# A streaming encoder step on one core: attention blocks transposed into other PSUM tiles, half of the weight differences on GpSimd, other steps and banks at the ends of the state-space loop

## The chip, the cores and the metric

The kernel is one program on one core of a Trainium2 chip. Its time is the device time of one execution in microseconds; the figure given for a version is the median of several executions. The engines are TensorE (PE, with its weight loads shown apart as PEld), VectorE (DVE), ScalarE (ACT), GpSimd (POOL) and SyncE (SP), which here issues nearly all DMAs. Each engine runs its own instructions strictly in the order of the program; a waiting instruction holds all behind it on its engine.

## The reference

It is one layer of a hybrid encoder, for 2048 frames of a new stream and 8 x 16 frames of running streams (17 tiles of 128 frames), in float32:

```
h = rms_norm(x) * gain
u, g_s, q, k, v, g_a = split(h @ w_in)            # w_in: 1024 x 3072
y_s = S5(u): 32 groups of 16 channels, each with a 64-dim complex diagonal state,
      a scan over the frames, y = Re(C h) + D u, gelu, then a GLU with w_glu (512 x 1024)
y_a = band attention: 8 heads x 64, q and k normed, each chunk of 64 frames sees itself
      and the 8 chunks before, bias by clipped distance; running streams attend a cache of 512
mixed = concat(y_s * silu(g_s), y_a * silu(g_a))
out = x + mixed @ w_out                           # w_out: 1024 x 1024
```

Returned are the outputs, the newest keys and values, and the final states.

## The kernel before

**Two streams of work.** `run` interleaves a foreground (the input projection `inproj` in three passes over the 17 tiles, then `glu`, then `outproj`) and a background (preparation of the state-space part, `s5`, `decode` for the running streams, `attention`). All are Python generators that write instructions as they go; each `yield` states a cost. For each foreground cost (650 for a step of three matmuls) the background earns that cost times a ratio (0.42 while `s5` runs, 0.75 in `decode`; in `attention` it is worked out so that it ends 64 steps before the foreground) and spends it on its own yields. While a burst of weight conversions is due (`busy`), the ratio is 0. So the order of instructions on each engine is fixed when the program is written, and a yield of the background is a count of foreground steps put between two of its pieces.

**Matmuls in three terms.** Each product of the foreground (`mm3`, lines 190 to 194) takes a float32 operand as a rounded high part and a low difference: high x high, high x low, low x high. The weights go through `conv_w` (line 145 on): a block of 128 x 512 is loaded by SP into one of five raw buffers (`NR`), ACT writes the rounded part `whi` (line 155, scaled by the norm's gain), DVE the difference `wlo` (line 156). The blocks of pass 1 and pass 2 are converted in a burst at the last tile of the pass before, 16 blocks at 1.25 steps each, and the load of the block five further on is issued two steps later (`T_LW`). Their first use is one step per block from the start of the new pass.

**q and k.** `ev_norm` has DVE sum the squares (`s`, line 280), POOL make a reciprocal root from it (lines 281 and 282), DVE scale (`zs`, line 285), and PE transpose the result into a PSUM tile `tr` (line 295). The one buffer of `tr` in the pool `pst` also holds the transposes of `glu` (line 1361).

**The state-space loop.** `s5` loads blocks of u (`load_u`, SP), reorders them on ACT (`perm_u`, line 720) and transposes them on PE (`step_a`, line 734); `feed(n)` loads block n+3, reorders block n+1 and transposes block n. The first of these follow the flag that pass 0 has stored u. In the loop DVE and ACT rotate and scan, POOL makes tables of cosines and sines, PE multiplies. At its end PE transposes the final states into a PSUM tile `ut` with one buffer, DVE copies them out (line 938) into a buffer `bt` with one, and SP stores them, behind eight stores of y (line 850).

**Attention.** 128 pieces: 16 units of two heads and four frames' tiles, two heads each, four tiles of queries. `qk` multiplies into the PSUM tile `s` and DVE adds the bias and takes the minimum; `soft` makes exponentials on ACT; `tr` transposes the weights by PE in blocks of 128 (up to five, line 1203) into the PSUM tile `pt`, which holds 8 blocks, two banks, one buffer; ACT writes their rounded part (`pth`, line 1210), DVE the difference (`ptl`, line 1211); `pv` multiplies with the values. Every fourth piece from the 12th on also brings a gate: `gate_b` transposes two blocks into the last two places of `pt`, and DVE multiplies (`mo`, line 1256). The list `post` holds DVE work back until the next yield is over. The PSUM pools of attention have one buffer for each tag (`bufs=1` is the default of `pool`), and with `s` (two banks), `pt` (two), `o` (one), `tr` (one) and the foreground's two all eight banks are in use.

**Glu.** For each tile SP loads the stored gate `gs` (line 1376), POOL multiplies it into `ms` (line 1402), and PE transposes that one tile later (line 1361).

Of the kernel before, what the change touches and what calls it, by code (L numbers as in the profile page):

```python
# [31 lines left out]
def fv(ap):  # L32
    return ap.bitcast(F32)
# [6 lines left out]
class Build:  # L40
# [101 lines left out]
    def conv_w(self):  # L142
        nc = self.nc
        n = self.nconv
        self.nconv += 1
        key, _, k = self.chunks[n]
        raw = self.raws.pop(n)
        hi = self.wp.tile([128, 512], F32R, tag="whi", name="whi", bufs=16)
        lo = self.wp.tile([128, 512], F32R, tag="wlo", name="wlo", bufs=16)
        if k is None:  # L150
            nc.scalar.activation(out=hi, in_=raw, func=AF.Copy)
            nc.vector.tensor_sub(lo, raw, fv(hi))
        else:
            gcol = self.gain[:, k:k + 1]
            nc.scalar.activation(out=hi, in_=raw, func=AF.Copy, scale=gcol)  # L155
            nc.vector.scalar_tensor_tensor(lo, raw, gcol, fv(hi), op0=OP.mult, op1=OP.subtract)  # L156
        self.W[key] = (hi, lo)
        if self.step:
            self.defer(self.T_LW, lambda: self.load_w(n + self.NR))
        elif n + self.NR < 16:  # L160
            self.load_w(n + self.NR)
        else:

            self.defer(40 + 10 * (n + self.NR - 16), lambda: self.load_w(n + self.NR))
# [286 lines left out]
    def s5(self):  # L451
# [257 lines left out]
        def load_u(b, i):  # L709
            c0, n = BLK[i]  # L710
            u = mp.tile([128, L, GB * CH], F32, tag="U", name="U", bufs=3)
            nc.sync.dma_start(u[0:n], u4[c0:c0 + n, :, b * GB * CH:(b + 1) * GB * CH])
            U[b, i] = u

        def perm_u(b, i):
            n = BLK[i][1]
            u = U.pop((b, i))
            o = mp.tile([128, GB, L, CH], F32, tag="P", name="P")
            src = u[0:n].rearrange("p j (g h) -> p g j h", g=GB)
            nc.scalar.activation(out=o[0:n], in_=src, func=AF.Copy)  # L720
            P[b, i] = o.rearrange("p g j h -> p g (j h)")
# [148 lines left out]
            yield None  # L870
        for n in range(3):
            load_u(0, n)
        yield 2 * SL
        perm_u(0, 0)
        yield SL
        for n in range(3):
            feed(n)
            yield SL
# [52 lines left out]
        nc.sync.dma_start(self.O["rp"], of[:, 0:64])  # L931
        nc.sync.dma_start(self.O["ip"], of[:, 64:128])
        for i in range(2):
            yield 1500
            pf = ps.tile([128, 128], F32, tag="ut", name="pf2")
            nc.tensor.transpose(pf, FINs[:, 4 * i:4 * i + 4].rearrange("p b g -> p (b g)"), self.ident)
            of = mp.tile([128, 128], F32, tag="bt", name="of2", bufs=1)
            nc.vector.tensor_copy(of, pf)
            nc.sync.dma_start(self.O["rs"][128 * i:128 * i + 128], of[:, 0:64])
            nc.sync.dma_start(self.O["is"][128 * i:128 * i + 128], of[:, 64:128])  # L940
# [163 lines left out]
    def attention(self):  # L1104
# [91 lines left out]
        def tr(x, gate):  # L1196
            n, s, a = x
            j0 = span(x)
            w = a + 5 - j0
            pr = PR.pop(x)  # L1200
            t = ps.tile([128, 8, 128], F32, tag="pt", name="pt")
            for k in range(w):
                nc.tensor.transpose(t[:, k], pr[:, 128 * k:128 * k + 128], self.ident)  # L1203
            if gate is not None:
                gate_b(gate, t[:, 6:8])
            if a == 0:
                PT[n, s] = [p.tile([128, 20, 128], F32R, tag=f"pt{y}", name=f"pt{y}", bufs=1) for y in "hl"]

            h, l = (v[:, 4 * a + j0:5 * a + 5] for v in PT[n, s])
            nc.scalar.activation(out=h, in_=t[:, 0:w], func=AF.Copy)  # L1210
            post.append(lambda: nc.vector.tensor_tensor(out=l, in0=t[:, 0:w], in1=fv(h), op=OP.subtract))  # L1211

        def pv(n, s, y):
            if y == 0:
# [26 lines left out]
        def gate_b(gate, t):  # L1241
            n, h = gate
            m, G = units[n]
            for a in range(2):
                nc.tensor.transpose(t[:, a], GT[n][:, 2 * h + a], self.ident)
            o = p.tile([128, 2, 128], F32, tag="mo", name="mo")
            ot = OT[n]
            P = 2 * G + h

            def put():  # L1250
                nc.sync.dma_start(self.mt_d[2 * P:2 * P + 2, :, 4 + m, :].rearrange("t p q -> p t q"), o)
                if m == 3:
                    self.flags["att", P] = True

            def mul():
                nc.vector.tensor_mul(o, ot[:, 2 * h:2 * h + 2], t)
                late.append(put)

            post.append(mul)

        subs = [(n, s, a) for n in range(len(units)) for s in range(2) for a in range(4)]
        SL = self.SL_ATT
# [18 lines left out]
        for i in range(N + 6):  # L1281
            self.att_left = N + 6 - i
            if i < N:
                x = subs[i]
                while not self.flags.get(("ga", 4 * units[x[0]][1] + 3)):
                    yield None
                qk(x)
                yield self.W_QT * SL
                flush()
            done = i >= 2 and subs[i - 2][2] == 3 if i - 2 < N else False  # L1290
            if done:
                n, s, a = subs[i - 2]
                pv(n, s, 0)
                if i < N:
                    soft(x)
                yield self.W_PV * SL
                flush()
                pv(n, s, 1)
                yield self.W_PV * SL
                flush()  # L1300

            gate = None
            if i % 4 == 0 and i >= 12 and i < N:
                gate = (i - 12) // 8, (i - 12) // 4 % 2
            elif i in tail:
                gate = tail[i]
            if 0 <= i - 1 < N:
                tr(subs[i - 1], gate)
                gate = None
                yield self.W_QT * SL  # L1310
                flush()
                self.use_spare()
            if gate is not None:
                gate_b(gate, ps.tile([128, 8, 128], F32, tag="pt", name="pt")[:, 6:8])
                yield self.W_QT * SL
                flush()
            if i < N and not done:
                soft(x)
            if i >= 8 and i % 8 == 0:
                gate_a(i // 8 - 1)  # L1320
            if i < N:
                n, r = x[0], i % 8
                if r == 2:
                    load_ga(n)
                if n + 1 < len(units) and r < 6:
                    loads(n + 1)[r]()
                if r == 3:
                    bias(2 * n + 2)
                if r == 5:
                    bias(2 * n + 3)  # L1330
# [22 lines left out]
    def glu(self):  # L1353
# [13 lines left out]
        for i, t in enumerate(TILES):  # L1367
# [5 lines left out]
                self.out_load(0)  # L1373
            hi, lo = self.GY.pop(t)
            g = self.ev.tile([128, 512], F32, tag="plain", name="gs")
            nc.sync.dma_start(g, self.gs_d[128 * t:128 * t + 128])
            z = {}
            for f in (1, 0):
                z[f] = self.psm.tile([128, 512], F32, tag="mm", name="z")
# [229 lines left out]
```

## Time and profile before

| | |
|---|---|
| median of 3 executions | 1228.99 us (1226.14 to 1230.14) |
| profiled execution | 1225.45 us, its span 1223.6 us |
| mean granted TensorE clock | 0.993 |
| PE busy | 97% |
| DVE busy | 58% |
| ACT busy | 50% |
| POOL busy | 30% |
| DMA, mean | 194 GB/s |

The profile is that of one execution. Busy time is the union of an engine's instructions; matmuls overlap in the pipeline and their ends are modelled, so a matmul is shown longer than the distance to the next one. "Idle before" is the time in which an engine did nothing ahead of an instruction, with what ended it. The granted clock is the share of TensorE's full clock that was given in a stretch.

### The profile page before, as it was taken

The numbers are of one execution on the slowest core, as the hardware profiler recorded it, in microseconds if no ns is written. First come the engines' busy times: TensorE is split into PE (matmuls) and PEld (weight loads), VectorE is DVE, ScalarE is ACT, GpSimd is POOL, SyncE is SP. The second block draws the span as 40 slices with busy tenths as digits, with TensorE's granted clock in tenths as the row PEclk, the third lists the DMA queues.
The fourth block names the chain that finished last, engine by engine and source line by source line (L and its number), as shares of the span: only waits on it lengthen the run. The fifth ranks groups of instructions, "written<-read, shape, count | busy, mean of one in ns | idle before, by whom it ended". The sixth has DMA issues, their size and how long they took to land.

```text
span 1223.6 us, 18141 instructions
## 1 busy us (share of the span) xinstructions
PE 1185.6 (97%) x6363; PEld 973.3 (80%) x6363; DVE 714.5 (58%) x1358; ACT 610.6 (50%) x1177; POOL 364.2 (30%) x407
## 2 busy tenths in 40 slices
PE   8999999899999999999899999999999999999998
PEld 6888888678788887787667878788788788888887
DVE  5476627489888888963234336665655555555511
ACT  6435436465555666553243446555655455555510
POOL 2433562267757647530000011111211111111120
PEclk9999999999999999999999999999999999999999
DMA  7765456757466778445796598998578687778143
GB/s 251 241 193 167 150 169 202 219 140 168 119 170 159 160 223 196 103 111 94 212 349 232 160 270 247 265 263 228 196 227 237 185 221 231 211 210 256 57 132 117
DMA packets 250018, 236.78 MB, mean 194 GB/s; under 512 B 111256, under 2 KB 184736, under 8 KB 248904
## 3 DMA queue, kind: packets, MB, share of 16 engines
q1 hardware_dynamic: 248408, 232.16, 66.4%
q0 software_dynamic: 1376, 3.47, 1.0%
q8 instruction: 50, 0.82, 0.3%
q14 instruction: 40, 0.33, 0.1%
q10 hardware_dynamic: 144, 0.00, 0.0%
HBM read 169.48 MB, written 68.06 MB: 194 GB/s over the span
## 4 chain that ended last, share of the span: by engine, by line
PE 78%; DMA 9%; DVE 5%; ACT 4%; SPq 3%; issue 2%; POOL 0%; DVEq 0%; ACTq 0%; POOLq 0%
PE z L192 18%; PE z L194 18%; PE z L193 18%; PE o L1221 5%; PE pt L1203 5%; PE s L1173 5%; DMA wraw<-in_w_in_dram 3%; PE pt L295 1%; PE v L772 1%; PE y L841 1%; PE y L840 1%; DMA mt<-mt_d 1%; PE o L1062 1%; DMA vc<-in_vc_dram 1%; DVE hlo L232 1%
## 5 line engine op out<-in xcount | busy, mean ns | idle before, releaser
L192 PE MATMUL z<-whi,hhi 128*128 128x512 f32 x816 | 342.0, 419 | 0.8 <-ACT whi L155 0.7
L193 PE MATMUL z<-wlo,hhi 128*128 128x512 f32 x816 | 321.1, 394 | 2.4 <-DVE wlo L156 2.4
L194 PE MATMUL z<-whi,hlo 128*128 128x512 f32 x816 | 320.9, 393 | 0.0
L192 PEld LDWEIGHTS z<-whi,hhi 128*128 128x128 f32 x816 | 154.5, 189 | 36.3 <-issue 3.3
L193 PEld LDWEIGHTS z<-wlo,hhi 128*128 128x128 f32 x816 | 154.5, 189 | 35.6 <-DVE wlo L156 6.1
L194 PEld LDWEIGHTS z<-whi,hlo 128*128 128x128 f32 x816 | 154.1, 189 | 33.7
L1210 ACT ACTIVATE pth<-pt 128x640 fp32r<-128x640 f32 (+4 forms) x128 | 81.7, 638 | 133.8 <-PE pt L1203 95.5
L1211 DVE TENSOR_TENSOR ptl<-pt,pth 128x640 fp32r<-128x640 f32 (+4 forms) x128 | 94.5, 739 | 54.2 <-ACT pth L1210 53.2
L1192 ACT ACTIVATE sn<-sn,mn 128x640 f32<-128x640 f32 (+4 forms) x128 | 96.9, 757 | 36.0 <-DVE mn L1183 34.1
L192 PE MATMUL z<-whi,mh 128*128 128x512 f32 x272 | 114.4, 420 | 0.0
L194 PE MATMUL z<-whi,ml 128*128 128x512 f32 x272 | 107.5, 395 | 0.0
L193 PE MATMUL z<-wlo,mh 128*128 128x512 f32 x272 | 107.2, 394 | 0.0
L1183 DVE CUSTOM_DVE_ANT_0 sn<-s,bias 128x640 f32<-128x640 f32 (+4 forms) x128 | 93.2, 728 | 7.2 <-PE s L1173 7.0
L1203 PE MATMUL pt<-ident,sn 128*128 128x128 f32 x560 | 83.1, 274 | 9.7 <-DVE ptl L1211 6.4
L1402 POOL TENSOR_TENSOR ms<-ms,gs 128x512 f32<-128x512 f32 x16 | 20.7, 1291 | 230.9 <-DMA gs<-gs_d 119.5
L1173 PE MATMUL s<-ks,q 128*128 128x320 f32 (+1 forms) x448 | 88.1, 313 | 0.2 <-DVE mn L1183 0.2
L1203 PEld LDWEIGHTS pt<-ident,sn 128*128 128x128 f32 x560 | 64.7, 140 | 29.5 <-ACT sn L1192 12.8
L1173 PEld LDWEIGHTS s<-ks,q 128*128 128x128 f32 x448 | 75.5, 189 | 13.1 <-DVE mn L1183 3.0
L1417 POOL TENSOR_TENSOR ml<-mt,mh 128x1024 fp32r<-128x1024 f32 x17 | 40.6, 2390 | 126.8 <-ACT mh L1416 95.1
L232 DVE TENSOR_TENSOR hlo<-xraw,hhi 128x1024 fp32r<-128x1024 f32 x49 | 60.8, 1241 | 20.7 <-ACT hhi L229 18.8
L1238 POOL TENSOR_TENSOR ga<-ga,sum 128x512 f32<-128x512 f32 x16 | 16.7, 1044 | 171.6 <-DVE sum L1236 123.6
L281 POOL TENSOR_SCALAR s<-s 128x8 f32<-128x8 f32 x34 | 15.1, 445 | 176.5 <-DVE s L280 176.1
(261 smaller groups left out, 2111.7 us busy)
## 6 DMA issues: line engine op xcount, KB each, us to landing
xraw<-in_xT_dram SPq DMA_DIRECT2D x49, 512.0 KB
q<-qt_d SPq DMA_DIRECT2D x64, 256.0 KB
ks<-kt_d SPq DMA_DIRECT2D x28, 512.0 KB
vhl<-vp_d SPq DMA_DIRECT2D x28, 512.0 KB
wraw<-in_w_in_dram SPq DMA_DIRECT2D x48, 256.0 KB
bias<-tl_d SPq DMA_DIRECT2D x32, 320.0 KB
mt<-mt_d SPq DMA_DIRECT2D x17, 512.0 KB
x<-in_x_dram SPq DMA_DIRECT2D x34, 256.0 KB
```

The costliest lines, as they stand in the source:

```text
L192: mm(z, a, whi, start=first, stop=False)
L193: mm(z, a, wlo, start=False, stop=False)
L194: mm(z, b, whi, start=False, stop=last)
L232: nc.vector.tensor_sub(lo, raw, fv(hi))
L1173: nc.tensor.matmul(ps_s[:, bank, 0:wp], Q[n, x2][:, s, 128 * a:128 * a + 128], KS[n][:, s, c0:c0 + wp], start=(x2 == 0), stop=(x2 == 1))
L1183: nc.vector.tensor_tensor_reduce(out=o, in0=i0, in1=i1, scale=1.0, scalar=3e38, op0=OP.add, op1=OP.min, accum_out=mn)
L1192: nc.scalar.activation(out=sn[:, 0:w], in_=sn[:, 0:w], func=AF.Exp, scale=-1.0, bias=mn, accum_out=SUM[n][:, a, s:s + 1])
L1203: nc.tensor.transpose(t[:, k], pr[:, 128 * k:128 * k + 128], self.ident)
L1210: nc.scalar.activation(out=h, in_=t[:, 0:w], func=AF.Copy)
L1211: post.append(lambda: nc.vector.tensor_tensor(out=l, in0=t[:, 0:w], in1=fv(h), op=OP.subtract))
L1221: nc.tensor.matmul(o[:, a0:a1], VB[n][:, j, s, :], t[:, 3 * a0 + j + a0:4 * (a1 - 1) + j + 1:4], start=(y == 0 and j == 4), stop=(y == 1 a ...
L1417: self.defer(2, lambda: self.nc.gpsimd.tensor_tensor(out=lo, in0=m, in1=fv(hi), op=OP.subtract))
```

## The change

Five edits: (1) at the start of the loop the first `perm_u` is written 5 SL after the loads instead of 2, and the first `feed` 2 SL after that instead of 1 (SL is 800). (2) For weight blocks of odd number in passes 1 and 2 the difference is made by POOL in two instructions, a scaling of the raw block in place and a subtraction. (3) At the end of the loop the two last state transposes use the PSUM tiles `y` and `v` and the buffers `VB` and `bt`, 2500 apart instead of 1500. (4) `gs` is loaded from POOL's queue. (5) In attention `pt` has four blocks; the fifth block and the gate's two go to the tile `tr` of `pst`; the fifth is rounded and subtracted first, its subtraction and the gate's product are written at once instead of held back.

```diff
@@ conv_w
-            nc.vector.scalar_tensor_tensor(lo, raw, gcol, fv(hi), op0=OP.mult, op1=OP.subtract)
+            if key[0] and n % 2:
+
+                nc.gpsimd.tensor_scalar(raw, raw, gcol, None, op0=OP.mult)
+                nc.gpsimd.tensor_tensor(out=lo, in0=raw, in1=fv(hi), op=OP.subtract)
+            else:
+                nc.vector.scalar_tensor_tensor(lo, raw, gcol, fv(hi), op0=OP.mult, op1=OP.subtract)
@@ s5, start of the loop
+        yield 5 * SL
+        perm_u(0, 0)
         yield 2 * SL
-        perm_u(0, 0)
-        yield SL
         for n in range(3):
             feed(n)
             yield SL
@@ s5, end
-            yield 1500
-            pf = ps.tile([128, 128], F32, tag="ut", name="pf2")
+            yield 2500
+            pf = ps.tile([128, 128], F32, tag=("y", "v")[i], name="pf2", bufs=2)
...
-            of = mp.tile([128, 128], F32, tag="bt", name="of2", bufs=1)
+            of = mp.tile([128, 128], F32, tag=("VB", "bt")[i], name="of2", bufs=(2, 1)[i])
@@ attention, tr
-            t = ps.tile([128, 8, 128], F32, tag="pt", name="pt")
-            for k in range(w):
+            v = min(w, 4)
+            t = ps.tile([128, 4, 128], F32, tag="pt", name="pt")
+            for k in range(v):
                 nc.tensor.transpose(t[:, k], pr[:, 128 * k:128 * k + 128], self.ident)
-            if gate is not None:
-                gate_b(gate, t[:, 6:8])
+            r = None
+            if w > v or gate is not None:
+                r = self.pst.tile([128, 4, 128], F32, tag="tr", name="pr")
+                if w > v:
+                    nc.tensor.transpose(r[:, 0], pr[:, 512:640], self.ident)
+                if gate is not None:
+                    gate_b(gate, r[:, 2:4])
...
-            h, l = (v[:, 4 * a + j0:5 * a + 5] for v in PT[n, s])
-            nc.scalar.activation(out=h, in_=t[:, 0:w], func=AF.Copy)
-            post.append(lambda: nc.vector.tensor_tensor(out=l, in0=t[:, 0:w], in1=fv(h), op=OP.subtract))
+            c0 = 4 * a + j0
+            parts = ([(c0 + 4, 1, r)] if w > v else []) + [(c0, v, t)]
+            for c, m, src in parts:
+                h, l = (x[:, c:c + m] for x in PT[n, s])
+                nc.scalar.activation(out=h, in_=src[:, 0:m], func=AF.Copy)
+
+                def low(h=h, l=l, src=src, m=m):
+                    nc.vector.tensor_tensor(out=l, in0=src[:, 0:m], in1=fv(h), op=OP.subtract)
+
+                if src is r:
+                    low()
+                else:
+                    post.append(low)
@@ attention, gate_b
-            post.append(mul)
+            mul()
@@ attention, the gates after the last piece
-                gate_b(gate, ps.tile([128, 8, 128], F32, tag="pt", name="pt")[:, 6:8])
+                gate_b(gate, self.pst.tile([128, 4, 128], F32, tag="tr", name="pr")[:, 2:4])
@@ glu
-            nc.sync.dma_start(g, self.gs_d[128 * t:128 * t + 128])
+            nc.gpsimd.dma_start(g, self.gs_d[128 * t:128 * t + 128])
```

## Rows read from the trace of the kernel before

**Rows 1.** The page's first part: busy us, share of the span, instructions.

```profile
PE 1185.6 (97%) x6363; PEld 973.3 (80%) x6363; DVE 714.5 (58%) x1358; ACT 610.6 (50%) x1177; POOL 364.2 (30%) x407
```

**Rows 2.** Waits of PE: line and releaser, total us, times, longest.

```profile
PE pt L1203 <- DVE ptl L1211: 6.4, 7, 1.1
...
PE ut L734 <- ACT P L720: 3.3, 1, 3.3
...
PE tm L1361 <- POOL ms L1402: 2.5, 1, 2.5
...
PE pf L936 <- DVE of L938: 2.3, 1, 2.3
PE v L772 <- DVE t L792: 2.3, 1, 2.3
```

**Rows 3.** Table by stretch: length, busy of five engines, granted clock, DMA share, GB/s.

```profile
224.00:229.00 5.00, 4.43 (x18) 3.75 (x18) 2.09 (x5) 4.88 (x8) 1.22 (x2) 0.66 1.01 310
714.00:720.00 6.00, 4.96 (x18) 3.53 (x18) 1.93 (x3) 2.12 (x4) 0.74 (x1) 0.72 1.04 348
```

**Rows 4.** The same table for a stretch without a wait.

```profile
594.00:606.00 12.00, 12.00 (x55) 9.93 (x54) 2.35 (x3) 3.48 (x5) 0.01 (x1) 1.00 0.87 223
```

**Rows 5.** Timeline near 216 to 220, PE and SP: start, us, instruction, idle before.

```profile
216.62 0.50 PE L193 MATMUL z<-wlo,hhi 128*128 128x512 f32 x1 [0.46 <-DVE wlo L156]
219.27 0.63 PE L295 MATMUL pt<-ident,zs 128*128 128x128 f32 x4 [1.93 <-DVE zs L285]
...
218.25 4.17 SPq L712 DMA_DIRECT2D U<-u_d  x3
```

**Rows 6.** POOL's groups by form: busy us, mean ns, idle before.

```profile
L288 POOL TENSOR_TENSOR plain<-zs,kgrow 128x512 f32<-128x512 f32 x5 | 6.4, 1287 | 7.8 <-ACT whi L155 3.4 <-DMA u_d<-plain 2.5 <-DVE zs L285 1.9
...
L648 POOL MEMSET T<- 128x512 f32 x2 | 1.0, 523 | 0.0
```

**Rows 7.** Timeline of ACT and POOL at the end of the first burst.

```profile
212.01 1.94 ACT L155 ACTIVATE whi<-wraw,gain 128x512 fp32r<-128x512 f32 x3
...
214.90 2.50 POOL L282 TENSOR_TENSOR s<-s,nhalf 128x8 f32<-128x8 f32 x1
```

**Rows 8.** DVE and POOL at 202.6, and DVE's group by form.

```profile
202.58 1.88 DVE L156 SCALAR_TENSOR_TENSOR wlo<-wraw,gain,whi 128x512 fp32r<-128x512 f32 x1
...
202.62 1.29 POOL L288 TENSOR_TENSOR plain<-zs,kgrow 128x512 f32<-128x512 f32 x1 [3.40 <-ACT whi L155]
...
L156 DVE SCALAR_TENSOR_TENSOR wlo<-wraw,gain,whi 128x512 fp32r<-128x512 f32 x48 | 35.8, 773 | 18.5 <-ACT whi L155 18.4
```

**Rows 9.** Timeline of DVE at the loop's end.

```profile
585.43 0.29 DVE L938 COPY of<-pf 128x128 f32<-128x128 f32 x1 [8.86 <-DMA out_dram<-of]
```

**Rows 10.** Timeline of SP, POOL and ACT at the first tiles of glu.

```profile
704.69 0.70 SPq L1376 DMA_DIRECT2D gs<-gs_d  x1
...
713.49 1.26 POOL L1402 TENSOR_TENSOR ms<-ms,gs 128x512 f32<-128x512 f32 x1 [119.47 <-DMA gs<-gs_d]
...
716.61 0.63 ACT L1349 ACTIVATE yh<-y 128x512 fp32r<-128x512 f32 x1 [9.17 <-DMA y<-y_d]
```

**Rows 11.** Groups by form of ACT and DVE in attention's transposes.

```profile
L1210 ACT ACTIVATE pth<-pt 128x640 fp32r<-128x640 f32 x96 | 67.7, 705 | 109.1 <-PE pt L1203 76.7 <-PE pt L1245 31.8
...
L1210 ACT ACTIVATE pth<-pt 128x512 fp32r<-128x512 f32 x8 | 4.8, 598 | 6.4 <-PE pt L1245 5.7 <-PE pt L1203 0.7
...
L1211 DVE TENSOR_TENSOR ptl<-pt,pth 128x640 fp32r<-128x640 f32 x96 | 79.0, 823 | 46.0 <-ACT pth L1210 45.2
...
L1211 DVE TENSOR_TENSOR ptl<-pt,pth 128x512 fp32r<-128x512 f32 x8 | 5.5, 684 | 0.0
```

**Rows 12.** Timeline of PE in attention, one of the seven waits.

```profile
861.09 0.74 PE L1203 MATMUL pt<-ident,sn 128*128 128x128 f32 x5 [0.95 <-DVE ptl L1211]
```

**Rows 13.** Waits of PE's weight loads: total us, times, longest.

```profile
PEld pt L1203 <- ACT sn L1192: 12.8, 32, 2.7
```

**Rows 14.** The table by stretch, first weight burst.

```profile
197.00:221.00 24.00, 21.62 (x99) 17.26 (x97) 18.00 (x24) 14.72 (x23) 7.57 (x6) 1.00 0.85 260
```

## The prediction

> **What bounds the kernel now.** I read the busy times first: PE 1185.6 us, 97% of the span [rows 1]. Little but PE's own idle time can be won, 38 us, so the next view is who PE waited for [rows 2], and then where each wait lies in the timeline. The waits that the change touches are few and single: 3.3 us for P at the start of the state-space loop, 2.5 us for the first gated product, 2.3 us for the last state transpose, 2.3 us for DVE after the second weight burst, and 6.4 us in seven waits of the attention's transposes for the difference that empties their PSUM tile. The table by stretch adds what the wait list hides: right after the long waits the granted clock is low, 0.66 over 5 us and 0.72 over 6 us [rows 3], part of the stretch at the 1.2 GHz level and the rest at 2.4. One minus the clock, times the length, is 0.34 x 5 = 1.7 and 0.28 x 6 = 1.7 us. There are five such stretches, all behind waits of over 2 us; each costs another 1.7 us. For converting delays: undisturbed PE starts some 53 matmuls in 12 us [rows 4], 0.227 us each, and a foreground step is three, 0.68 us.
>
> **Change 1, the loop's start (5 SL ahead of the first perm_u, 2 SL after).** At 218.25 SP issues the loads of U, and PE then sits idle 3.3 us for the copy P made from them [rows 2, 5]. The new yields put 4 x 800 = 3200 cost units more between load and use; the background earns 650 x 0.42 = 273 a step, so 11.7 steps, 8 us of PE work. That covers the 3.3 us: 3.3 us gained, and 1.7 of clock if nothing else stops PE there. Nothing is added; the whole loop runs 8 us later under the same foreground.
>
> **Change 2, half the weight differences on GpSimd (16 pairs, 8 in each of the two bursts at the ends of passes 0 and 1).** Removed from DVE: 8 instructions a burst. Added on POOL: a scaling in place and a subtraction each. The subtraction has a row of its own shape, 1.29 us; the scaling has none: below it lies the memset of that tile size, 0.52, above it the two-input 1.29 [rows 6]. I take 0.7, since it reads one tensor, near the memset: a pair is 2.0 us, bounds 1.8 to 2.6. What counts is POOL's queue at the end of a burst. Burst one: the rounding of blocks 11 to 13 starts at 212.01 on ACT, 1.94 for three, so block 11 is there at 212.7. POOL then does its pair (to 214.7), the two norm instructions queued behind it (2.50 us for the power alone [rows 7], with the scaling before it 3, to 217.7), pair 13 (to 219.7) and pair 15 (to 221.7). PE wanted difference 13 at 216.16, where it waited 0.46 us for DVE, and then 1.93 for zs, 2.4 in all [rows 5]. Now it waits 3.6 us for pair 13, zs hides behind that, and some 0.5 us for pair 15: 4.1, so +1.7, and one low-clock stretch stays, +1.7 against change 1. Together with change 1: -5.0 + 3.4 = -1.6; bounds -7.4 (every wait there goes) to +2 (pairs of 2.6: three in the chain, 0.6 each, and difference 15 too). Burst two: DVE no longer stands behind block 15's load, but zs then waits for POOL's power behind pair 11, at about the old time; I take 0, bounds -4.0 (2.3 and the clock) to +4. Raw buffers come free later where POOL frees them; the next load of such a buffer is five blocks on, so I cost it at nothing; if it isn't covered, it is in the upper bound.
>
> A rule that speaks against this edit: DVE's instruction at 202.58 took 1.88 us, where a POOL instruction started at 202.62 beside it; its group's mean is 0.77 [rows 8]. The Trainium skill (SBUF — State Buffer, section SBUF: two separate sides) says that VectorE and GpSimd share one pair of ports as an exclusive lock, taken by a two-input VectorE instruction or a GpSimd one for its whole length. By that row the trace agrees; by the rule in full the sum is that of rival (a), 1231.8, by the queue alone 1221.8.
>
> **Change 3, the loop's end (other PSUM banks and buffers, 2500 for 1500).** SP issues eight stores of y first, the small outputs queue behind, DVE's copy stands 8.86 us for the buffer's store, and PE 2.3 us for the PSUM tile that the copy frees [rows 2, 9]. The new tiles were last used long before (VB) or have two buffers (y, v), and the second copy, in the old buffer, comes 5000/273 = 18 steps, 12 us, later, when the store that ended near 585.4 is over. -2.3 and -1.7: -4.0; bounds -4.0 to 0. The two yields make decode and attention begin another 7 steps later.
>
> **Change 4, gs on POOL's queue.** SP issues the first gs at 704.69 behind a row of others; POOL's product starts at 713.49 on its landing, and PE waits 2.50 us [rows 2, 10]. POOL is idle there, so the load goes off as soon as its buffer is free, and does not stand behind SP's earlier transfers. -2.5, and -1.7 for the clock, with 0.2 of the wait next to it: -4.4. What is late next is y: ACT waited 9.17 us for it, to 716.61 [rows 10]. Its cover now: the attention's first loads, which shared the queues with it, come about 19 steps (13 us) later. Bounds -4.4 to 0.
>
> **Change 5, the attention's blocks.** The words of the change speak of two alternating banks, but the pool has one buffer for each tag, and pt is asked for without a count: it stays one tile, now of one bank, and its next writer still waits for its reader. Per step ACT does 512 columns and 128 in place of 640: 0.598 + 0.277 (0.598 less three times the 0.107 that the two rows differ by for a block), in place of 0.705, partly overlapped when back to back; the difference shrinks from 0.823 to 0.684 [rows 11]. The tile is free about 0.15 us earlier in a wait that has five blocks, like that at 861.09 [rows 12]; I take four of the seven, -0.6 of the 6.4. The exponential behind it on ACT starts near 0.08 later, and the next transposes' weight loads wait for that 32 times [rows 13], 2.6 at most; most of these are short, so I take a quarter, +0.6. At the 32 gates DVE's product now goes first and ACT's copy of the shared tile behind it, but the two products of `pv` lie before the next use, so I cost that at nothing; if they don't cover it, it is in the upper bound. New is the third tile, shared with the foreground's transposes: where those follow at once, they wait for a copy (0.28), a difference (0.27) and the signals, some 0.9 us. About five tiles of the foreground overlap with five-block steps; I take two, +1.8, bounds 0 to 4.5. Attention is squeezed by 19 of some 344 steps (1224 in all, less 816 of the projection and the 64 of the margin), 5%: I take +1, bounds 0 to 3. Sum +2.8, bounds -1 to +8.
>
> **Sum.** -1.6 + 0 - 4.0 - 4.4 + 2.8 = -7.2 us against the profiled execution, 1225.45 us (1223.6 and 1.85 around it). That lies 3.5 below the median of the runs shown, 1228.99, so I put the difference on the median: 1221.8.
>
> **Rivals.** (a) GpSimd and DVE block each other in the bursts: slower. As at 202.58, each of 16 POOL instructions costs DVE up to 1.88 - 0.77 = 1.1 us, 17.6, less 8 x 0.77 = 6.2 relieved: 11 us more DVE work in a burst of 24 us where DVE is 18 us busy [rows 14], 5 us too late; both bursts, +10: 1231.8. It decides against the change when about 70% of those meetings are paid. For it: that row. Against: POOL is busy 7.6 of those 24 us now, so many pairs meet an idle DVE. The lock of the Trainium skill's page SBUF — State Buffer (section SBUF: two separate sides) makes it the full price. (b) The first gated product's wait is handed to y (ACT stands for y until 716.61 anyway), and the shared tile takes its share: 1221.8 + 4.4 = 1226.2, no change. For it: the 9.17 us wait. Against: the traffic moves away. (c) The bursts come clean, since DVE is no longer held by blocks that have not arrived: change 2's 3.4 is not paid, the 2.4 it left goes, and 4.0 in burst two: 1212.0. Two real banks in attention would also land here, -6.4.
>
> **Chances.** Forecast 0.50, (a) 0.15, (b) 0.20, (c) 0.15. Range 1212 to 1231, the forecast's own 1217 to 1226. A difference of 0.3%, 3.7 us, is about what can be told from none. Faster: 0.43 of the forecast, 0.07 of (b), all of (c), 0.65. Within: 0.22. Slower: 0.13, nearly all (a).
>
> **What would show it.** PE's waits for P, for the state copy and for the first gated product gone from the wait list, and the granted clock near 1.00 at 580 to 600 and 700 to 720; a wait of PE for a POOL difference of some 3 to 4 us near 216; pt waits for the difference still there at some 5 us; tm behind the shared tile's reader. The prediction is wrong if the POOL pairs run well over 2.6 us or the wait at the first burst is below 1 us, if the pt waits vanish (two banks), or if the attention's 128 pieces take over 5 us more together.

## The result and the profile after

The changed kernel took 1233.38 us (median of 7 executions, 1232.39 to 1236.79), the kernel before beside it 1226.55 us (median of 7): ratio 1.0053, 95% interval 1.0039 to 1.0068. It is 6.5 us slower. The forecast was 0.9942 (1221.8 us), so the kernel moved the other way, and its time lies outside the stated range of 1212 to 1231 us.

First the busy line of the page after, which answers to [rows 1], and then the list of who PE waited for, which answers to [rows 2]. POOL is busy 63 us longer; PE has the same matmuls.

```profile
span 1230.9 us, 18401 instructions
...
PE 1183.0 (96%) x6363; PEld 969.1 (79%) x6363; DVE 727.7 (59%) x1438; ACT 617.8 (50%) x1273; POOL 427.4 (35%) x456
```

```profile
PE z L198 <- POOL wlo L159: 18.7, 10, 4.2
PE pt L1210 <- ACT sn L1197: 5.2, 6, 1.7
PE pt L1210 <- DVE ptl L1228: 4.4, 6, 1.4
PE s L1178 <- DVE mn L1188: 3.4, 1, 3.4
...
PE ut L739 <- ACT kr L700: 1.4, 1, 1.4
```

The waits for P, for the state copy and for the first gated product are gone. In their place stands one line that the kernel before has not: 18.7 us for differences made by POOL, 9.2 in the first burst and 9.5 in the second. POOL's groups by form say what one costs: 1.90 and 1.41 us, 3.3 for the pair.

```profile
L158 POOL TENSOR_SCALAR wraw<-wraw,gain 128x512 f32<-128x512 f32 x16 | 30.4, 1903 | 2.6 <-ACT whi L155 2.4
...
L159 POOL TENSOR_TENSOR wlo<-wraw,whi 128x512 fp32r<-128x512 f32 x16 | 22.6, 1413 | 1.3
```

The table by stretch (columns as in [rows 3]) shows that the stretches near 580 to 600 and 700 to 720 are now at a granted clock of 1.00, where the kernel before has 0.91 in both. Behind the two bursts the clock is 0.91, as it was before; what has grown there is PE's idle time. First the changed kernel:

```profile
220.00:240.00 20.00, 15.76 (x66) 12.58 (x67) 6.32 (x10) 6.00 (x10) 11.54 (x9) 0.91 0.80 242
460.00:480.00 20.00, 11.37 (x42) 7.74 (x40) 11.45 (x13) 10.71 (x20) 19.41 (x13) 0.91 0.62 185
580.00:600.00 20.00, 20.00 (x89) 16.32 (x89) 4.36 (x6) 6.34 (x11) 0.00 (x0) 1.00 0.35 98
700.00:720.00 20.00, 20.00 (x93) 16.46 (x92) 8.36 (x14) 9.72 (x17) 3.04 (x4) 1.00 0.86 268
```

The same stretches of the kernel before:

```profile
220.00:240.00 20.00, 16.71 (x75) 13.29 (x74) 6.06 (x11) 9.30 (x18) 2.99 (x4) 0.91 0.84 242
460.00:480.00 20.00, 17.68 (x82) 13.79 (x81) 19.11 (x30) 14.46 (x32) 16.69 (x19) 0.91 0.84 168
580.00:600.00 20.00, 17.68 (x72) 14.15 (x71) 5.30 (x9) 5.69 (x8) 0.96 (x1) 0.91 0.58 111
700.00:720.00 20.00, 17.25 (x73) 13.29 (x71) 6.87 (x11) 5.90 (x11) 1.26 (x1) 0.91 0.95 263
```

The timeline of POOL in the first burst: it hardly stops from 198.47 on. The pair of block 13 starts at 222.37, behind block 11's and the norm's power, and PE stood 4.24 us for it, to 225.85. Three waits of PE for pairs 7, 9 and 11 (1.66, 1.25 and 2.07 us) lie ahead of it. The last row is PE's.

```profile
213.24 1.57 POOL L158 TENSOR_SCALAR wraw<-wraw,gain 128x512 f32<-128x512 f32 x1
214.89 1.26 POOL L159 TENSOR_TENSOR wlo<-wraw,whi 128x512 fp32r<-128x512 f32 x1
216.13 1.57 POOL L158 TENSOR_SCALAR wraw<-wraw,gain 128x512 f32<-128x512 f32 x1
217.78 2.10 POOL L159 TENSOR_TENSOR wlo<-wraw,whi 128x512 fp32r<-128x512 f32 x1
219.97 0.20 POOL L286 TENSOR_SCALAR s<-s 128x8 f32<-128x8 f32 x1
220.25 2.12 POOL L287 TENSOR_TENSOR s<-s,nhalf 128x8 f32<-128x8 f32 x1
222.37 2.08 POOL L158 TENSOR_SCALAR wraw<-wraw,gain 128x512 f32<-128x512 f32 x1
224.53 1.26 POOL L159 TENSOR_TENSOR wlo<-wraw,whi 128x512 fp32r<-128x512 f32 x1
...
225.85 0.66 PE L198 MATMUL z<-wlo,hhi 128*128 128x512 f32 x1 [4.24 <-POOL wlo L159]
```

A pair also holds the raw buffer until its subtraction is over, and SP's next load into that buffer waits for it. SP's queue has its own list of waits; these are its lines for weight loads (L139) that waited for a difference of the bursts, in the changed kernel and then in the kernel that differs only by having all differences on DVE (e1 below). Seven of the eight loads that follow a pair of the first burst go off within 0.03 us of the end of POOL's subtraction.

```profile
SPq L139 <- POOL wlo L159: 33.1, 12, 5.0
```

```profile
SPq L139 <- DVE wlo L156: 10.8, 17, 1.6
```

### The profile page after: what moved, and what is told of

Same layout as the page of the kernel before. It is cut to its first block, busy times and chain, and to the rows that moved or that the text cites. A ratio compares the mean times of both kernels' runs of the same rounds, so it can differ in the third digit from the quotient of the medians.

```text
span 1230.9 us, 18401 instructions
## 1 busy us (share of the span) xinstructions
PE 1183.0 (96%) x6363; PEld 969.1 (79%) x6363; DVE 727.7 (59%) x1438; ACT 617.8 (50%) x1273; POOL 427.4 (35%) x456
## 4 chain that ended last, share of the span: by engine, by line
PE 84%; DMA 5%; ACT 3%; POOL 3%; issue 2%; DVE 2%; SPq 0%; POOLq 0%; DVEq 0%; ACTq 0%
PE z L197 21%; PE z L199 20%; PE z L198 20%; PE o L1243 5%; PE s L1178 5%; PE pt L1210 4%; DMA wraw<-in_w_in_dram 2%; POOL wraw L158 1%; DMA mt_d<-mo 1%; PE pt L300 1%; PE y L845 1%; PE y L846 1%; PE v L777 1%; PE o L1067 1%; PE pr L1215 1%
## 5 line engine op out<-in xcount | busy, mean ns | idle before, releaser
L198 PE MATMUL z<-wlo,hhi 128*128 128x512 f32 x816 | 321.6, 394 | 20.8 <-POOL wlo L159 18.7
L198 PEld LDWEIGHTS z<-wlo,hhi 128*128 128x128 f32 x816 | 154.1, 189 | 57.9 <-POOL wlo L159 23.6
L1228 DVE TENSOR_TENSOR ptl<-pt,pth 128x512 fp32r<-128x512 f32 (+3 forms) x128 | 81.8, 639 | 19.3 <-ACT pth L1225 19.1
L1225 ACT ACTIVATE pth<-pt 128x512 fp32r<-128x512 f32 (+3 forms) x128 | 70.9, 554 | 24.7 <-PE pt L1210 24.6
L1210 PE MATMUL pt<-ident,sn 128*128 128x128 f32 x464 | 72.8, 275 | 9.8 <-ACT sn L1197 5.2
L1225 ACT ACTIVATE pth<-pr 128x128 fp32r<-128x128 f32 x96 | 26.7, 278 | 106.0 <-PE pr L1215 64.3
L1210 PEld LDWEIGHTS pt<-ident,sn 128*128 128x128 f32 x464 | 54.3, 140 | 29.3 <-ACT sn L1197 9.9
L237 DVE TENSOR_TENSOR hlo<-xraw,hhi 128x1024 fp32r<-128x1024 f32 x49 | 62.8, 1282 | 22.9 <-ACT hhi L234 21.1
L1253 DVE TENSOR_TENSOR ot<-o,tmp 64x512 f32<-64x512 f32 x32 | 22.0, 689 | 75.3 <-ACT tmp L1251 75.3
```

What stands on the lines that cost most here:

```text
L198: mm(z, a, wlo, start=False, stop=False)
L1225: nc.scalar.activation(out=h, in_=src[:, 0:m], func=AF.Copy)
L1228: nc.vector.tensor_tensor(out=l, in0=src[:, 0:m], in1=fv(h), op=OP.subtract)
```

## The experiments

Ratios are to the kernel before, run on the same chip in the same session (its medians 1223 to 1225 us); 0.001 is 1.2 us. Diffs are against the changed kernel where not said otherwise.

**All differences on DVE (e1).**

```diff
-            if key[0] and n % 2:
-                nc.gpsimd.tensor_scalar(raw, raw, gcol, None, op0=OP.mult)
-                nc.gpsimd.tensor_tensor(out=lo, in0=raw, in1=fv(hi), op=OP.subtract)
-            else:
-                nc.vector.scalar_tensor_tensor(lo, raw, gcol, fv(hi), op0=OP.mult, op1=OP.subtract)
+            nc.vector.scalar_tensor_tensor(lo, raw, gcol, fv(hi), op0=OP.mult, op1=OP.subtract)
```

> The changed kernel with all 32 scaled weight differences of the bursts back on DVE. Theory T (the price of the change is GpSimd's pair: scaling 1.90 us and subtraction 1.41 us, together 3.3 us where I had taken 2.0, so that POOL is late in both bursts): the 18.7 us that PE waits in the two bursts fall to the 4.7 they were before or less, and the two low-clock stretches there mostly go; the other parts of the change keep their gain. About 1219 us, ratio to the kernel before 0.993 to 0.996. Rival R1 (the attention edit or the shifted loop ate the gain, the bursts only moved the waiting): 1229 or more. A port lock between the engines (rival R2) expects here the same as T.

0.9955 (0.9937 to 0.9973). Change 2 costs 1.0053 - 0.9955 = 0.0098, 12.0 us; the rest of the change gains 5.5 us, not the 10.6 that its terms give (-5.0 - 4.0 - 4.4 + 2.8).

**Change 2 alone, on the kernel before (e2).** The diff is that of `conv_w` ahead of the prediction.

> The kernel before with nothing but the half of the weight differences put on GpSimd. T: the bursts cost what they cost in the changed kernel, some 14 us more than on DVE, less what the wait for P hides of it: 1237 to 1241. Rival R1: the edit alone costs at most a few us, under 1232, and the loss needs the rest of the change.

1.0112 (1.0089 to 1.0134), +13.7 us. The price is there without the other edits: R1 falls.

**A cheaper scaling: on ACT (e3), as a two-input product on GpSimd (e8).**

```diff
-                nc.gpsimd.tensor_scalar(raw, raw, gcol, None, op0=OP.mult)
+                nc.scalar.activation(out=raw, in_=raw, func=AF.Copy, scale=gcol)                                    # e3
+                nc.gpsimd.tensor_tensor(out=raw, in0=raw, in1=gcol.to_broadcast([128, 512]), op=OP.mult)           # e8
```

> The changed kernel with the in-place scaling of the odd blocks moved from GpSimd to ACT, behind the block's rounding; GpSimd keeps the 16 subtractions. T: a block costs POOL 1.4 us in place of 3.3 and ACT some 0.65 more, so POOL is not late any more; the waits of PE in the bursts fall below 6 us together: 1219 to 1223. R2 (POOL and DVE hold each other up by a shared lock, so each POOL instruction on a tensor of that size costs much the same): half of the POOL instructions are left, so at least a third of the loss of the bursts stays: 1225 to 1229, and the POOL subtractions or DVE's differences beside them run clearly above 1.3 and 0.8 us.

> The changed kernel with GpSimd's scaling written as a two-input product of the block and its gain column spread over the 512 columns, in place of the one-input scaling by a column. T (the price of GpSimd's scaling itself): the scaling takes the 1.3 us that two-input products of that size take there, the pair 2.6 to 2.8 us, so that the waits for the differences fall from 18.7 us to 10 to 13 and the kernel lands 4 to 7 us below the changed one, ratio to before 0.999 to 1.002. R2 (meetings with DVE set the duration, whatever the instruction): the scaling stays near 1.9 us and the ratio at 1.004 to 1.006.

e3: 1.0016 (1.0001 to 1.0031), 1226.95 us: a miss for T, and inside the range of R2 (1225 to 1229). R2's sign is there too, though small: the subtraction takes 1.38 us in the mean, and DVE's difference 0.87 where e1 has 0.77. e8: 1.0024 (1.001 to 1.0038), 3.6 us better than the changed kernel. Its groups by form show the two-input product at 1.27 us where the one-input scaling took 1.90, and its waits for POOL fell from 18.7 to 12.6 us, as T expected, though the ratio is just above T's 0.999 to 1.002; R2, which had the scaling stay near 1.9 us, falls here. But in e3, with no scaling on POOL at all, 7.7 us of such waits stayed, 2.76 us of them for a subtraction that stood behind the norm's power: the size of the pair is not the whole price. The rows are e8's.

```profile
L159 POOL TENSOR_TENSOR wlo<-wraw,whi 128x512 fp32r<-128x512 f32 x16 | 24.8, 1550 | 1.3
L158 POOL TENSOR_TENSOR wraw<-wraw,gain 128x512 f32<-128x512 f32 x16 | 20.3, 1270 | 3.0 <-DMA wraw<-in_w_in_dram 2.9
```

**Half of the pairs: the first eight blocks of a burst (e12), the last eight (e14).**

```diff
-            if key[0] and n % 2:
+            if key[0] and n % 2 and n % 16 < 8:     # e12
+            if key[0] and n % 2 and n % 16 >= 8:    # e14
```

> The changed kernel with GpSimd's pairs only for the odd blocks among the first eight of a burst (4 of 8 pairs, none behind the norm's power in GpSimd's queue); the last eight blocks all on DVE. T (a queue too long for the burst, 8 x 3.3 us and the norms in it, and the late blocks behind the power): the queue is short of the deadline and nearly all of the loss goes, 0.9955 to 0.998, with under 2 us of waits for GpSimd's differences. R2 (each meeting of GpSimd and DVE costs): half of the loss stays, about 1.0005.

> The changed kernel with GpSimd's pairs only for the odd blocks among the last eight of a burst; of the buffers that come free late there, one is needed again in the burst. Theory L: the roundings on ACT end when they do with all differences on DVE, and only the pairs of blocks 13 and 15 behind the norm's power are waited for, some 4 us a burst where 2 to 3 of it replace the wait for zs: 0.997 to 1.000. Theory Q: as much of the loss as with the first half or more, 1.002 to 1.004.

e12: 1.0032 (1.0016 to 1.0048), above what both theories expected. e14: 1.0024 (1.0012 to 1.0036), inside Q's range and beyond L's, though L was right that the roundings end when they do with DVE alone. Either half keeps most of the loss against e1 (9.4 and 8.5 of 12.0 us), so they are not halves of one price. My theory of a queue that is too long fell with e12 as the whole account: POOL was done with its four pairs at 214, and yet PE waited 4.6 us for POOL's differences in the two bursts (T had under 2), and then 3.49 us for zs on DVE, where e1 has 1.81. The groups on the tile of the raw block tell the two apart; the row of ACT's roundings gives the start of the first and of the last in the first burst. For e1, the changed kernel, e12 and e14, in this order:

```profile
L155 ACT ACTIVATE whi<-wraw,gain x16: 707/721/727, 198.1 to 216.4; 128x512 fp32r<-128x512 f32 x16
```

```profile
L155 ACT ACTIVATE whi<-wraw,gain x16: 703/722/727, 197.0 to 221.9; 128x512 fp32r<-128x512 f32 x16
```

```profile
L155 ACT ACTIVATE whi<-wraw,gain x16: 707/722/725, 197.8 to 222.1; 128x512 fp32r<-128x512 f32 x16
```

```profile
L155 ACT ACTIVATE whi<-wraw,gain x16: 712/720/728, 199.6 to 218.2; 128x512 fp32r<-128x512 f32 x16
```

The burst lasts 18.3 us with DVE alone, 24.9 in the changed kernel, 24.3 with the early pairs and 18.6 with the late ones. The other kernels with all differences on DVE and loads as before lie between 18.5 and 19.8. The second burst, in the same order, lasts 22.6, 25.3, 25.1 and 22.9. Early pairs stretch the burst. SP's queue in e12 shows how: three loads take SP from 199.83 to 203.49, where POOL's first pair ends at 202.66, and four from 210.71 to 215.14, where POOL's last pair ends at 214.00. SP issues in order, so the loads behind such a one wait too: the buffer of block 2 is free at 200.90, and its load goes off at 203.07, behind the one that waited for POOL. What makes PE wait in the end is DVE's order: the scaling of zs stands there behind the difference of the burst's last block, which was rounded at 222.1.

```profile
199.83 3.66 SPq L139 DMA_DIRECT2D wraw<-in_w_in_dram  x3
...
206.08 0.80 SPq L139 DMA_DIRECT2D wraw<-in_w_in_dram  x2
...
210.71 4.43 SPq L139 DMA_DIRECT2D wraw<-in_w_in_dram  x4
```

In e1 the same rows are 1.65 us at 200.14 and 3.12 us at 205.63. Late pairs leave the burst as it was, and stand behind the power on POOL. This is e14's timeline of POOL; PE waited 4.13 us for the pair that ends at 223.3, and 3.67 us in the second burst for the like (4.22 in the changed kernel):

```profile
217.60 0.52 POOL L286 TENSOR_SCALAR s<-s 128x8 f32<-128x8 f32 x1
218.20 1.68 POOL L287 TENSOR_TENSOR s<-s,nhalf 128x8 f32<-128x8 f32 x1
219.87 2.09 POOL L158 TENSOR_SCALAR wraw<-wraw,gain 128x512 f32<-128x512 f32 x1
222.04 1.26 POOL L159 TENSOR_TENSOR wlo<-wraw,whi 128x512 fp32r<-128x512 f32 x1
```

**Late loads without GpSimd (e13).** e1 with one number changed, three steps of 0.68 us.

```diff
-    T_LW = 2
+    T_LW = 5
```

> The changed kernel with all differences on DVE, and each weight block's next load asked for three foreground steps (2.0 us) later than now; no GpSimd in the bursts' weights. Theory L (raw buffers that come late carry the loss: load, 4.4 us to landing, rounding and difference form a chain of three links over a burst of 16 blocks and 5 buffers): each link 1.5 us longer, 4 to 5 us at the end of a burst, so that the kernel goes from 0.9955 to 1.000 to 1.004, and ACT's roundings wait for the loads more. Theory Q (GpSimd's queue alone): the slack of the loads takes it, 0.9945 to 0.997.

1.009 (1.0071 to 1.0109): 16.5 us more than e1 for 2.0 us put in, and beyond what either theory expected. PE's longest waits are again for zs, 5.58 and 6.77 us, one in each burst, as the last weight blocks come late and DVE has their differences ahead of zs. The row of roundings runs from 198.5 to 222.6, as in the changed kernel, with DVE doing all the differences:

```profile
L155 ACT ACTIVATE whi<-wraw,gain x16: 710/722/726, 198.5 to 222.6; 128x512 fp32r<-128x512 f32 x16
```

So late loads alone can make a loss of this size. Not all of it lies in the bursts: the loads of the later weights are late too. PE has the same instructions in the same order in these kernels, so their profiled executions can be compared by foreground steps. Against e1, the thirty steps around the first burst take longer by 10.4 us in the changed kernel, 7.8 in e12, 6.6 in e14, 7.7 in e13 and 4.4 in e3; the 35 steps around the second by 4.5, 2.6, 1.8, 4.7 and 3.6. Kernels that have the same code there differ by up to 3.1 us at the first burst (e1, with 23.4 us, is the shortest of them) and 1.0 at the second.

A sixth raw buffer was not tried. The nearest to buffers freed earlier while GpSimd still makes the differences is e3: the first six odd blocks hold theirs 2.8 to 3.2 us from the rounding on, where the changed kernel holds them 4.3 to 7.6. SP's waits for POOL's subtractions fall from 33.1 to 13.5 us, the first burst lasts 19.6 us, as with DVE alone, and 4.5 us are gained; 7.5 us of the loss stay. So the held buffers are a cause, but not the only one, and how the 12.0 us divide between them, the pairs behind the power and the meetings of POOL and DVE isn't shown: e12 and e14 together lose more than the changed kernel.

**The other parts, each alone on the kernel before (e5 the loop's ends, e6 gs, e7 attention), and together (e10 ends and gs).** The diffs are those ahead of the prediction.

> The kernel before with only the edits at the two ends of the state-space loop (wider yields at its start; other banks, buffers and yields for the small outputs at its end); weight differences, gs and attention as before. My forecast put change 1 at -5.0 and change 3 at -4.0: -9.0, ratio 0.9927. After the first runs the theory is: the waits for P (3.3 us) and for the state copy (2.3) go and part of the clock comes back, -5 to -9. Rival R1 (the later loop and the squeezed attention take the gain back): within 2 us of the kernel before, 0.9985 to 1.0015.

> The kernel before with only the load of gs moved from SP's queue to GpSimd's. Forecast: -4.4 us (2.5 of wait, 1.7 of clock, 0.2 beside it), ratio 0.9964. Rival (b) of the prediction: the wait is handed on to y, within 1 us of before, ratio 0.999 to 1.001, with a wait of PE behind ACT's yh near 713 to 717 in place of the one for the product.

> The kernel before with only the attention's edit (one-bank tile pt, the fifth block and the gate blocks in the third tile that the foreground shares, the gate's product at once). Forecast for the same without the squeeze: +1.8 us (bounds -1 to +5), ratio 1.0015. If the sum of the other parts is as forecast (-13.4 with the bursts on DVE) and the first run's loss of 5 to 6 us against it lies here: +6 to +8, ratio 1.005 to 1.0065.

> The kernel before with the loop's ends and gs on GpSimd, attention and weight differences as before. If the attention's edit costs its 7 us here too, as it did alone: 7 us under the kernel with all three (0.9955), 0.988 to 0.991. If its price hangs on where the foreground's transposes meet it in the shared tile (alone 3.3 us in three waits, with the ends 0.8 in one): within 2 us of the kernel with all three, 0.994 to 0.997. If the ends need the attention's edit: about 0.997, as the ends alone.

e5: 0.9972 (0.9957 to 0.9987). e6: 1.0027 (1.0012 to 1.0041). e7: 1.0058 (1.0039 to 1.0077). e10: 0.9971 (0.996 to 0.9983). e5 falls short of its -5 to -9 us, e6 is slower than either of its theories, e7 is where its second sum put it, and e10 where its third case did (the ends need the attention's edit). Alone the three sum to +7.0 us, together (e1) they are -5.5: their prices hang on where foreground and background meet. Four things are seen.

First, the ends alone end the wait for the gated product: in e5 it is not in the list, gs still on SP. On POOL without the ends (e6) it grows from 2.5 to 5.4 us. The timeline of POOL shows why: the second gs load, which waits for a store from its buffer, stands ahead of the first product.

```profile
701.98 0.59 POOL L1376 DMA_DIRECT2D gs<-gs_d  x1 [103.36 <-DMA gs_d<-plain]
720.40 0.55 POOL L1376 DMA_DIRECT2D gs<-gs_d  x1 [17.84 <-DMA gs_d<-plain]
720.97 1.27 POOL L1402 TENSOR_TENSOR ms<-ms,gs 128x512 f32<-128x512 f32 x1
```

Second, the attention's edit alone brings the collision that the prediction named, `PE tm L1378 <- DVE ptl L1223`, 3.3 us in three waits; with the ends (e1) it is 0.8 in one. Third, with the ends but the old attention (e10) PE's waits for ptl grow from 6.4 to 9.2 us, and 3.8 us of new waits appear near 1166, where the output projection wants its input (mh and ml). With the new attention (e1) the first are 4.4 us and the second gone, while the waits for ACT's exponential grow from 0.8 to 5.4.

Fourth, the later loop lengthens the second weight burst, with all differences on DVE: 19.7 us before, 22.9 in e5 (19.3 and 19.6 in e6 and e7, which lack the ends). SP's rows show what moved. Before, eight loads of T end at 433.38 and the burst's first rounding is at 443.0; its first load goes off 0.03 us after its buffer is free. In e5 the first rounding is at 438.5, the loads of T end at 440.16, and the burst's first load goes off at 442.72, behind them and 2.1 us after its buffer is free. PE then waits 3.49 us for zs, where the kernel before has no such wait in this burst. The first two rows are of the kernel before, the others of e5.

```profile
427.48 5.90 SPq L701 DMA_DIRECT2D T<-kr  x8
...
445.05 4.24 SPq L139 DMA_DIRECT2D wraw<-in_w_in_dram  x5
```

```profile
434.19 5.97 SPq L701 DMA_DIRECT2D T<-kr  x8
...
442.72 3.15 SPq L139 DMA_DIRECT2D wraw<-in_w_in_dram  x5
```

Not all of the 12.5 us between +7.0 and -5.5 is placed by this: executions also differ by up to 3 us in a stretch that none of these edits touches (the first 240 foreground steps, 177.5 us in e10 and 180.5 in e4).

**gs back on SP, with the ends (e9), and with two real banks (e11).**

```diff
-            nc.gpsimd.dma_start(g, self.gs_d[128 * t:128 * t + 128])
+            nc.sync.dma_start(g, self.gs_d[128 * t:128 * t + 128])
```

> The changed kernel with all weight differences on DVE and the load of gs back on SP's queue; loop ends and attention as changed. Theory G (gs on GpSimd's queue was never the gain: the ends of the loop alone already removed the wait for the first gated product, and on GpSimd's queue the second gs load, waiting for its buffer, stands ahead of the first product): not slower than the kernel that differs only by gs on GpSimd (0.9955), 0.992 to 0.9965. The forecast's change 4 (that edit gives 4.4 us): 0.998 to 1.000, with PE waiting 2 us or more for the first product again.

> The fastest kernel so far (differences on DVE, two real buffers for the attention's transposed weights, 0.9912) with gs back on SP's queue. Theory G: the same or better, 0.988 to 0.992. The forecast's change 4: slower by 2 to 4 us, 0.993 to 0.995.

e9: 0.9964 (0.9949 to 0.9979), beside 0.9955 for e1; e11: 0.9928 (0.9904 to 0.9953), beside 0.9912 for e4. e9 is inside the range of theory G, e11 between its two. The intervals overlap in both pairs: by the medians gs on POOL is worth 1 to 2 us here, not clear of nothing, and PE's wait for the first gated product comes back in neither.

**Two real banks (e4), and loads one step earlier (e15).**

```diff
-            t = ps.tile([128, 4, 128], F32, tag="pt", name="pt")
+            t = ps.tile([128, 4, 128], F32, tag="pt", name="pt", bufs=2)     # e4, e15, with e1's conv_w
-    T_LW = 2
+    T_LW = 1                                                                 # e15
```

> The first of these kernels with two real buffers for the attention's transposed weights, so that two tiles of one bank each alternate (the changed kernel has one). If the 4.4 us in six waits for the difference that empties the tile are on the path: 2 to 4 us below the first of these kernels, 1215 to 1217, and those waits gone. If ACT's exponential or the shared tile come late instead: the same as the first within 1.5 us.

> The fastest kernel so far (differences on DVE, two real buffers for the attention's transposed weights, 0.9912) with each weight block's next load asked for one foreground step after its rounding in place of two. Theory L in proportion (three steps later cost 16.5 us, so one step earlier gives up to 5): 0.986 to 0.990, first to last rounding of the first burst under 18 us. If the buffer's release by DVE's difference sets the load already: the same as without, 0.9895 to 0.993.

e4: 0.9912 (0.9888 to 0.9935), 5.3 us under e1, a little more than expected; the waits for ptl are gone from its list. e15: 0.9882 (0.9861 to 0.9903), 1210.08 us, the fastest of all and faster than both kernels by more than the intervals. Its interval overlaps e4's, so the gain over e4 isn't clear of noise; but its first burst is 17.0 us long where e4's is 19.5 (200.6 to 220.1), its second 20.5 where e4's is 23.6, as the chain of loads asks, and its waits for zs are 3.7 us where e4 has 6.6:

```profile
L155 ACT ACTIVATE whi<-wraw,gain x16: 712/716/727, 196.6 to 213.6; 128x512 fp32r<-128x512 f32 x16
```

## Why the prediction was wrong

The changed kernel lies 13.6 us above the forecast (1.0053 against 0.9942). Change 2 makes 8.6 of it (12.0 measured by e1, +3.4 in the sum when change 1's -5.0 is taken out of the -1.6), the other parts 5.1.

- **The step that failed: "Raw buffers come free later where POOL frees them; the next load of such a buffer is five blocks on, so I cost it at nothing".** Five blocks are 6.25 steps, 4.3 us. The landing of a load alone took 3.7 to 4.6 us (e1, e12, the changed kernel), and with DVE's difference the buffer is free 1.5 us or more after the start of its rounding, so there was no slack at all: ACT waits 4.3 us for loads in the first burst of e1 already, and 10.5 in that of the changed kernel. SP's loads waited 33.1 us for POOL's subtractions. By the forecast the early pairs cost nothing; e12, which has only these, loses 9.4 us to e1 and shows the longer burst, and e13 makes one of that length by late loads alone. The text offered the upper bound to cover this step, but its bound, +2 for burst one and +4 for burst two, was drawn from POOL's queue only.
- **The scaling, 0.7 us taken, 0.52 to 1.29 as bounds: 1.90 measured**, outside both. "It reads one tensor, near the memset" was the error: of [rows 6] even the upper end was too low, and the pair of 3.3 us meets the text's own sign of being wrong (well over 2.6). Beside the 1.27 us of the two-input product in e8, the one-input form with a column as its scalar is the slower one. e8 puts the price of this at 3.6 us.
- **POOL's queue at the end of burst one: right as a mechanism.** The wait for pair 13 behind the power, forecast at 3.6 us, was 4.24 in the changed kernel and 4.13 in e14, though with pairs of 3.3 us. As a sum it was too small: 9.2 us of waits for POOL in the burst, where I had 4.1, since PE waited for pairs 7, 9 and 11 as well. **In burst two it was wrong:** I took 0, and the changed kernel waits 9.5 us there, 4.22 of it for the pair behind the power. The late pairs alone (e14) lose 8.5 us to e1, where the sum has 3.4 for all.
- **Change 1 and change 3: the waits went as forecast** (P 3.3, state copy 2.3; the clock 1.00 at 580 to 600), the time did not: -9.0 forecast, -3.4 alone. 1.3 us for kr took the place of P, the waits for zs grew from 3.7 to 6.6 and those for ptl from 6.4 to 9.5 us in e5. In the second burst the loads of T now stand ahead of the weight loads, and that burst is 3.2 us longer; near 1168 PE waits 3.7 us for the output projection's input. A later loop moves what meets what, and I priced the move only for attention's length.
- **Change 4: wrong.** The wait that it was to remove was removed by the loop's ends (e5); "the load goes off as soon as its buffer is free" overlooked that POOL itself stands for the buffer, and the product behind it (e6). Rival (b) had the size (about nothing), with another cause.
- **Change 5: pt is one tile, as read.** The pt waits were 4.4 us (forecast some 5), the shared tile 0.8 behind a difference and 0.8 behind the gate's product (forecast 1.8 in two). By e10 and e1 the edit gained 2 us with the ends, intervals overlapping; alone it cost 7.1. Two banks, put at 6.4 us, gave 5.3 (e4 beside e1), where 4.4 us of these waits were left to win.
- **Rival (a) came out near the time, but not by its mechanism.** POOL and DVE did slow each other, and POOL the more. Six of its 16 scalings took 1.57 us; the ten at whose start a DVE instruction was running, or began within 0.04 us, took 2.0 to 2.65. By the means that is 16 x 0.33 = 5.4 us more on POOL over both bursts, and 16 x 0.15 = 2.4 for the subtractions (1.41 us, the shortest 1.26). DVE's difference took 0.815 us in the mean where e1 has 0.772: 32 x 0.043 = 1.4 us more on DVE in all, not 11 a burst. The Trainium skill (SBUF — State Buffer, section SBUF: two separate sides) has one of the two blocked for the other's whole instruction. The trace shows the contention but not that price: three of DVE's differences, at 216.87, 456.99 and 466.37, ran wholly inside a scaling of 1.57 us and took 0.75 us. e13 shows the same long burst with no GpSimd in it. So the meetings are a part of the pair's 3.3 us; the price of rival (a) is not there.

## What to carry to other kernels

Before an operation is moved to a slower engine, look at which buffers it holds: if the time from one use of a buffer to the next hardly covers the load's landing, a later release comes back at every turn of the ring (in e13 loads asked for 2.0 us later made a burst of some three turns 5.8 us longer), and an in-order DMA queue hands it to the buffers behind it. A bound for an instruction that the trace doesn't show is to reach beyond the nearest rows, above all on POOL, where the scaling of one tensor by a column took longer than the product of two. Several edits that shift the phase of two interleaved streams don't add: the three other parts were +7.0 us one by one and -5.5 together, so such a change is measured whole and then with one part taken out.

## What the runs showed of the hardware

- POOL's scaling of 128x512 by a column, one tensor read, took 1.57 us when no DVE instruction ran at its start, even where one began later, and 2.0 to 2.65 when one did (six and ten of the 16 in the changed kernel). The product of two tensors of that size, the column spread over the row, took 1.27 us in the mean (e8).
- DVE's difference of that size took 0.75 us wholly inside such a scaling, three times in the changed kernel; the longest of those in the bursts took 1.38 us.
- A load asked for on POOL's queue holds POOL while its buffer is not free: 17.84 us ahead of the second gs load in e6.
